# One class of a head's keys and queries loaded and split a slot earlier, in a hybrid RG-LRU and dilated-attention block

## The chip, the cores and the metric

One core of one Trainium2 chip. The metric is the device time of one execution in microseconds (us). Engines are named as in the profile: PE (matmuls) with PEld (its weight loads), DVE, ACT, POOL, and SP, which here only issues DMAs. A change of less than 0.2% (about 4.3 us) is taken as no change.

## The reference

The block is one decoder layer over 2048 positions of width 1024, in float32. Only the attention branch matters here:

```python
DILATED_GROUPS = ((128, 1), (512, 4), (2048, 16))       # window, dilation; 8 heads of 128
h = rms_norm(x, g_norm[l]) * (1.0 + scale[:, None, :]) + shift[:, None, :]
x_rnn, z_rnn, q, k, v, z_attn, g_r, g_a = jnp.split(h @ w_in[l], IN_SPLITS, axis=-1)
...
def dilated_attention_mixture(q, k, v):
    outs, lses = [], []
    for window, dilation in DILATED_GROUPS:
        o, l = dilated_window_attention(q, k, v, window, dilation)   # banded causal softmax
        outs.append(o); lses.append(l)
    w = jax.nn.softmax(jnp.stack(lses, axis=0), axis=0)
    return jnp.einsum("gbsh,gbshd->bshd", w, jnp.stack(outs, axis=0))
...
y_attn = (o * jax.nn.silu(z_attn)) @ w_out_attn[l]
merged = jax.nn.sigmoid(g_r + bg_r) * y_rnn + jax.nn.sigmoid(g_a + bg_a) * y_attn
x = x + gate[:, None, :] * (merged @ w_o[l])             # then a final rms_norm
```

## The kernel before

Every float32 matmul is made of three: an operand is **split** into a high part, a copy rounded to the matmul's format (`hi_act` on ACT, line 160, or `hi_dve`, line 163), and a low part, the difference (`lo_pool` on POOL, line 166, or `lo_dve`, line 169). `mm3` (line 152) then multiplies high with high, high with low and low with high.

The program runs in stages: input projections and the recurrent branch; the attention with the output projection interleaved; then the last products. The change lies in the attention stage. It works on 16 heads (two halves f of the sequence, 8 heads h each), numbered here 0 to 15, and the instruction order of every engine is the order of the code. Time is cut into **slots**. A head has six units, one a slot: four "c" units (a residue class r of the positions modulo 4) and two "w" units (the undilated window), in the order c0, w0, c1, w1, c2, c3. A head starts at its slot B, the next head at B + 6. In each slot the PE does the scores of one unit, then steps of the output projection (the **fill**, matmuls `pj<-yh,S` and `pj<-yl,S`), the transposes of the unit seven slots back, more fill, and the weighted sums of the unit eight slots back:

```python
run(s, HEAD)
...                                   # scores of this slot's unit (PE)
softmax()                             # row minima and exponentials (DVE, ACT)
run(s, SOFTMAX)
owed = spend(fill, owed, rate * 2 / 3)
run(s, EXCHANGE)
owed = spend(fill, owed, rate / 3)
run(s, WEIGHTS)
...                                   # transposes (PE); copies from PSUM and lows (ACT or DVE)
owed = spend(fill, owed, 0.0)
...                                   # weighted sums (PE)
run(s, TAIL)
```

HEAD, SOFTMAX, EXCHANGE, WEIGHTS and TAIL are the five places of a slot at which a head's other work is put, by `at(slot, place, function)` in `enlist`.

The work around the change, for a head that starts at slot B:

- `load_kq(c)` (line 1422) loads the keys and queries of class c into a buffer `kraw` (four of them), by SP's DMA queue.
- `split_kq(c)` splits them into the tile `kq`, of which there is one for all heads; class c is its part c. The high is ACT's (128x512 in the first half, 128x768 in the second), the low POOL's.
- `window_queries(0)` (line 1436), at (B, HEAD), makes two casts on POOL, high and low, of queries of all four classes into the tile `q`. The first "w" unit's scores (matmuls `sc<-kq,q`, slot B + 1) read it.
- `gather` (line 1630), at WEIGHTS of the old head's last slot, is four small ACT instructions that write `sm`. The PE exchanges those statistics between partitions in the next slot (`sc<-sm,msk`), between two score groups. DVE and ACT then work out weights `M` (lines 1648 to 1674).
- `scale` (line 1542) multiplies a unit's probabilities `pp` by `M` on ACT, at the TAIL before the unit's transposes (lines 1562 and 1575, `pT<-cs,pp`).
- `split_v` and `split_v1` split values (`vh`, `wh`) at TAIL, high on ACT and low on POOL; the fill's own operands `yh`, `yl` are split on DVE and POOL. `load_v` and `load_v1` (lines 1442, 1460) load values into three `vraw` buffers.

Of the kernel before, what the change touches and what calls it, by code (L numbers as in the profile page):

```python
# [90 lines left out]
def decoder_block(ctx, tc, x, c, positions, g_norm, w_mod, b_mod, w_in, b_gate, conv_w, conv_b,  # L91
# [1308 lines left out]
    HEAD, SOFTMAX, EXCHANGE, WEIGHTS, TAIL = range(5)  # L1400
    plan, due = {}, []

    def at(slot, place, fn, *args):
        plan.setdefault((slot, place), []).append((fn, args))
# [5 lines left out]
    class Head:  # L1410
# [283 lines left out]
                stored.add((self.f, self.h, i))  # L1694

        def enlist(self, B):
            for c, (ld, s, place) in enumerate(((5, 2, HEAD), (5, 2, SOFTMAX), (4, 1, HEAD), (3, 0, HEAD))):
                at(B - (ld if B else 5), TAIL, self.load_kq, c)
                at(B - s, place, self.split_kq, c)
            at(B, HEAD, self.window_queries, 0)  # L1700
            at(B + 1, EXCHANGE, self.window_queries, 1)
            e = B + NU
            at(e - 1, WEIGHTS, self.gather)
            at(e, HEAD, due.append, self.exchange)
            at(e, SOFTMAX, self.exchange_alone)
            at(e, SOFTMAX, self.maxima)
            at(e, SOFTMAX, self.exponentials)
            at(e, WEIGHTS, self.weights)
            for u, (kind, x) in enumerate(ORDER):
                s = B + u + LAG  # L1710
                at(s - 1, TAIL, self.scale, kind, x)
                at(s - 1, TAIL, self.split_v if kind == "c" else self.split_v1, x)
                at(s - 3, TAIL, self.load_v if kind == "c" else self.load_v1, x)
            e = B + NU + LAG
            at(B + LAG - 1, TAIL, self.load_gate)
            at(e, TAIL, self.merge, 1)
            at(e + 1, TAIL, self.merge, 3)
            at(e + 2, TAIL, self.store)
# [498 lines left out]
```

## Time and profile before

| what | value |
|---|---|
| time, median of 3 runs (range) | 2168.0 us (2166.8 to 2169.54) |
| the profiled execution, its span | 2169.62 us, 2167.8 us |
| mean granted PE clock | 0.998 |
| busy, share of the span: PE, PEld, DVE, ACT, POOL | 99%, 82%, 69%, 60%, 51% |
| attention stage, from the first load of `kraw` to the last scores | 1345 to 1831 us |
| DMA | 521.39 MB, mean 241 GB/s |

A row of the timeline gives start, duration, engine, line, operation, output<-inputs, shapes, how many like it follow each other, and in brackets the idle time of the engine before it with what ended it. A matmul's end is modelled: matmuls follow each other faster than their durations say, so short waits of the PE don't show as idle time. A busy PE is therefore not a PE at its peak.

### The profile page before, as it was taken

To read this page: it belongs to the slowest core of one execution; us is meant where nothing else is said; L and a number is where in the kernel's file an instruction comes from. 1 tells how busy PE (TensorE), PEld (TensorE's weight loads), DVE (VectorE), ACT (ScalarE), POOL (GpSimd) and SP (SyncE) were. 2 spreads that over 40 slices of the span, in tenths; PEclk is the share of its full clock that TensorE was granted. 3 is DMA by queue.
4 is the path that set the end of the run, shared out by engine and by line. 5 is a ranking of instruction groups with operands and counts; after the bars stand their busy time and mean duration, and the time that the engine had idled before them with its cause. 6 is when DMAs were issued, how large, how long until landed. Compare 5 with 4: busy or idle time off the path is not lost.

```text
span 2167.8 us, 32585 instructions
## 1 busy us (share of the span) xinstructions
PE 2138.3 (99%) x10539; PEld 1787.8 (82%) x10539; DVE 1488.1 (69%) x2606; ACT 1296.9 (60%) x2591; POOL 1111.2 (51%) x868
## 2 busy tenths in 40 slices
PE   9999999999999999999999999999999999999998
PEld 6888778888888888888888887888888988878886
DVE  6759878768656725544536584687777787788887
ACT  5748668668644527457548532677878877444333
POOL 1467667777666323223234564466666564422444
PEclk9999999999999999999999999999999999999999
DMA  8467887886655378898996666988887777899553
GB/s 302 144 208 259 277 290 264 285 296 237 175 112 165 108 250 281 295 312 299 323 327 220 163 163 198 288 266 266 269 267 230 242 241 223 298 316 295 183 171 111
DMA packets 416431, 521.39 MB, mean 241 GB/s; under 512 B 107558, under 2 KB 282882, under 8 KB 415236
## 3 DMA queue, kind: packets, MB, share of 16 engines
q1 hardware_dynamic: 376244, 401.65, 59.7%
q10 hardware_dynamic: 34384, 99.78, 12.1%
q0 software_dynamic: 5632, 17.88, 2.6%
q8 instruction: 83, 1.36, 0.3%
q14 instruction: 88, 0.72, 0.1%
HBM read 332.02 MB, written 187.17 MB: 240 GB/s over the span
## 4 chain that ended last, share of the span: by engine, by line
PE 63%; DVE 5%; DMA 5%; POOL 3%; issue 3%; ACT 1%; SPq 1%; POOLq 0%; ACTq 0%; DVEq 0%
PE X L152 13%; PE V L152 13%; PE pj L152 8%; PE Z L152 7%; PE W L152 6%; PE Y L152 6%; PE sc L152 3%; PE o L152 3%; PE pg L152 1%; DMA fg<-mrT 1%; PE pT L1562 1%; POOL kq L166 1%; PE pT L1575 1%; DMA fg<-gaT 1%; DMA oT<-zt 1%
## 5 line engine op out<-in xcount | busy, mean ns | idle before, releaser
L166 POOL TENSOR_TENSOR S<-R,S 128x512 fp32r<-128x512 f32 x192 | 294.3, 1541 | 170.0 <-ACT S L160 87.3
L152 PE MATMUL V<-T,S 128*128 128x512 f32 x1344 | 324.2, 390 | 2.3 <-DVE ev L455 2.3
L152 PE MATMUL X<-T,S 128*128 128x512 f32 x1344 | 323.8, 390 | 1.5 <-ACT u L385 1.3
L152 PE MATMUL pj<-yh,S 128*128 128x512 f32 x896 | 322.1, 403 | 1.3 <-DVE fg L1786 0.8
L152 PEld LDWEIGHTS V<-T,S 128*128 128x128 f32 x1344 | 251.8, 188 | 56.3 <-issue 2.1
L152 PEld LDWEIGHTS X<-T,S 128*128 128x128 f32 x1344 | 251.7, 188 | 56.4 <-ACT u L385 3.0
L166 POOL TENSOR_TENSOR S<-s,S 128x512 fp32r<-128x512 f32 x116 | 170.6, 1471 | 151.1 <-ACT S L160 114.9
L152 PEld LDWEIGHTS pj<-yh,S 128*128 128x128 f32 x896 | 168.5, 188 | 32.6 <-DVE S L169 1.6
L1475 ACT ACTIVATE pp<-pp,st 128x256 f32<-128x256 f32 (+3 forms) x256 | 133.7, 523 | 73.1 <-DVE st L1474 71.7
L152 PE MATMUL pj<-yl,S 128*128 128x512 f32 x448 | 175.9, 393 | 0.6 <-POOL yl L166 0.3
L160 ACT ACTIVATE S<-s 128x512 fp32r<-128x512 f32 x124 | 77.4, 624 | 145.4 <-DVE s L285 91.0
L152 PE MATMUL W<-T,S 128*128 128x512 f32 x672 | 161.6, 389 | 0.0
L152 PE MATMUL Y<-T,S 128*128 128x512 f32 x672 | 161.5, 389 | 0.0
L152 PE MATMUL Z<-T,S 128*128 128x512 f32 x672 | 161.4, 389 | 0.0
L160 ACT ACTIVATE S<-R 128x512 fp32r<-128x512 f32 x200 | 121.6, 623 | 59.0 <-DMA R<-in_w_in_dram 14.8
L169 DVE TENSOR_TENSOR ptl<-pT,pth 128x384 fp32r<-128x384 f32 (+1 forms) x160 | 97.9, 628 | 76.0 <-ACT pth L160 73.7
L152 PEld LDWEIGHTS W<-T,S 128*128 128x128 f32 x672 | 126.0, 188 | 26.9 <-issue 0.9
L152 PEld LDWEIGHTS Z<-T,S 128*128 128x128 f32 x672 | 126.1, 188 | 26.2
L152 PEld LDWEIGHTS Y<-T,S 128*128 128x128 f32 x672 | 126.1, 188 | 26.1
L974 DVE SCALAR_TENSOR_TENSOR xc<-xr,par,xc 128x512 f32<-128x512 f32 x96 | 104.4, 1087 | 58.1 <-ACT xc L968 55.9
L166 POOL TENSOR_TENSOR s<-R,s 128x512 fp32r<-128x512 f32 x32 | 43.2, 1351 | 189.5 <-ACT s L160 173.0
L1542 ACT ACTIVATE pp<-pp,M 128x256 f32<-128x256 f32 (+3 forms) x256 | 117.9, 522 | 22.3 <-DVE M L1674 22.3
(417 smaller groups left out, 4922.8 us busy)
## 6 DMA issues: line engine op xcount, KB each, us to landing
sD<-S ACTq DMA_DIRECT2D x140, 512.0 KB, 3.8
S<-sD SPq DMA_DIRECT2D x140, 512.0 KB, 5.2
S<-wD SPq DMA_DIRECT2D x82, 512.0 KB, 5.6
R<-in_w_in_dram SPq DMA_DIRECT2D x144, 256.0 KB, 3.4
wD<-s ACTq DMA_DIRECT2D x64, 256.0 KB, 5.3
kraw<-kqT SPq DMA_DIRECT2D x32, 384.0 KB, 5.4
T<-in_w_mod_dram SPq DMA_DIRECT2D x16, 512.0 KB, 9.1
vN<-ev SPq DMA_DIRECT2D x32, 256.0 KB, 2.7
```

The lines of the kernel that those rows point to most:

```text
L152: nc.tensor.matmul(o, lhsT=l, rhs=r, start=st, stop=sp, **kw)
L160: nc.scalar.activation(o, i, AF.Copy)
L166: nc.gpsimd.tensor_tensor(o, i, h.bitcast(F32), ALU.subtract)
L169: return nc.vector.tensor_tensor(o, i, h.bitcast(F32), ALU.subtract).ins
L974: nc.vector.scalar_tensor_tensor(xc, xr[:, i : i + CH], cw(i), xc, ALU.mult, ALU.add)
L1475: nc.scalar.activation(pdst, pdst, AF.Exp, bias=m_, scale=-1.0, accum_out=l_)
L1542: nc.scalar.activation(pp, pp, AF.Copy, scale=w)
L1562: nc.tensor.transpose(pt[:, c0 + j * P : c0 + (j + 1) * P], pp[i][:, k * P : (k + 1) * P], ident)
L1575: nc.tensor.transpose(pt[:, c * P : (c + 1) * P], pp[:, half * P : (half + 1) * P], ident)
```

## The change

```diff
         def enlist(self, B):
-            for c, (ld, s, place) in enumerate(((5, 2, HEAD), (5, 2, SOFTMAX), (4, 1, HEAD), (3, 0, HEAD))):
+            for c, (ld, s, place) in enumerate(((5, 2, HEAD), (5, 2, SOFTMAX), (4, 1, HEAD), (4, 1, EXCHANGE))):
                 at(B - (ld if B else 5), TAIL, self.load_kq, c)
                 at(B - s, place, self.split_kq, c)
```

Class 3 of a head's keys and queries is loaded at the TAIL of slot B - 4 instead of B - 3, and split at EXCHANGE of slot B - 1 instead of at HEAD of slot B. Nothing is added or removed; for head 0 the load stays where it was, and no engine's order changes there. The order of PE and DVE is the same throughout.

On ACT, at the border between heads 13 and 14 (the high copy of class 3 is the `kq` row whose source is `kraw_17871` before and `kraw_17784` after; `pp,st` rows are the exponentials of slot B - 1 above and of slot B below). Before:

```order
L1475 ACTIVATE pp_17958,st_17537<-pp_17958,st_17537 128x512
L1630 ACTIVATE sm_17976<-st_17537,cs_60 128x2x16 x4
L160 ACTIVATE pth_17986<-pT_17981 128x512
L160 ACTIVATE pth_17994<-pT_17990 128x384
L1542 ACTIVATE pp_17467<-pp_17467,M_17557 128x384
L1542 ACTIVATE pp_17467<-pp_17467,M_17557 128x512
L160 ACTIVATE vh_18027<-vraw_17869 128x512
L160 ACTIVATE kq_12048<-kraw_17871 128x768
L1475 ACTIVATE pp_18051,st_18041<-pp_18051,st_18041 128x384
```

And now:

```order
L1475 ACTIVATE pp_17958,st_17537<-pp_17958,st_17537 128x512
L160 ACTIVATE kq_12048<-kraw_17784 128x768
L1630 ACTIVATE sm_17978<-st_17537,cs_60 128x2x16 x4
L160 ACTIVATE pth_17988<-pT_17983 128x512
L160 ACTIVATE pth_17996<-pT_17992 128x384
L1542 ACTIVATE pp_17467<-pp_17467,M_17557 128x384
L1542 ACTIVATE pp_17467<-pp_17467,M_17557 128x512
L160 ACTIVATE vh_18029<-vraw_17871 128x512
L1475 ACTIVATE pp_18051,st_18041<-pp_18051,st_18041 128x384
```

The high copy moved ahead of the gather, the copies of transposes, the scales and a value's high copy; the exponentials of slot B have lost it from in front of them.

On POOL at the same border, from class 2's low to the two casts of `window_queries(0)`. Before:

```order
L166 TENSOR_TENSOR kq_12048<-kraw_17782,kq_12048 128x768
L166 TENSOR_TENSOR yl_18006<-R_3429_17838,yh_18005 128x512
L166 TENSOR_TENSOR vh_18027<-vraw_17869,vh_18027 128x512
L166 TENSOR_TENSOR kq_12048<-kraw_17871,kq_12048 128x768
L1436 CAST q_3473_18037<-kq_12048 128x512 x2
```

And now:

```order
L166 TENSOR_TENSOR kq_12048<-kraw_17782,kq_12048 128x768
L166 TENSOR_TENSOR kq_12048<-kraw_17784,kq_12048 128x768
L166 TENSOR_TENSOR yl_18008<-R_3430_17840,yh_18007 128x512
L166 TENSOR_TENSOR vh_18029<-vraw_17871,vh_18029 128x512
L1436 CAST q_3473_18037<-kq_12048 128x512 x2
```

Class 3's low moved ahead of the fill's low and the value's low; the casts have the same instructions ahead of them as before, in another order. On SP the class 3 load stands right behind class 2's, ahead of the other loads of the slot between.

## The prediction

> **What bounds the kernel.** I read the page first, then the stage by windows, the PE's waits in it, the stage's tiles, and last the timeline at the borders between heads.
>
> ```profile
> PE 2138.3 (99%) x10539; PEld 1787.8 (82%) x10539; DVE 1488.1 (69%) x2606; ACT 1296.9 (60%) x2591; POOL 1111.2 (51%) x868
> ```
>
> ```profile
> 1345.00:1840.00 495.00, 485.98 (x3138) 433.87 (x3137) 367.94 (x1066) 381.70 (x1075) 293.99 (x255) 1.00 0.81 256
> ```
>
> The PE is the bound: it is idle for 29.5 us of the span and for 9.0 us of the 495 us of the attention stage (columns: PE, PEld, DVE, ACT, POOL, clock, DMA share). Nothing here can gain more than its waits. Of the PE's waits in that stage these two bear on the change (total, times, longest):
>
> ```profile
> PE sc L152 <- POOL q L1436: 4.6, 5, 1.7
> PE pT L1562 <- ACT pp L1542: 1.0, 2, 0.7
> ```
>
> The first is the wait at which the change aims: a head's first window scores wait for the two casts of the window queries, which stand behind class 3's low. The second is the next in line: transposes that wait for probabilities scaled by the weights M. What the moved pieces cost (min/median/max ns):
>
> ```profile
> L160 ACT ACTIVATE kq<-kraw x64: 614/730/843, 1350.9 to 1803.6; 128x512 fp32r<-128x512 f32 x32, 128x768 fp32r<-128x768 f32 x32
> L166 POOL TENSOR_TENSOR kq<-kraw,kq x61: 1282/1837/2310, 1355.7 to 1805.1; 128x768 fp32r<-128x768 f32 x32, 128x512 fp32r<-128x512 f32 x29
> L1436 POOL CAST q<-kq x60: 603/616/1078, 1378.4 to 1812.2; 128x512 fp32r<-128x512 f32 x60
> ```
>
> **The waits that can go.** The border into head 14 is the worst. First PE, then ACT, POOL and DVE there:
>
> ```profile
> 1763.88 0.38 PE L152 MATMUL sc<-sm,msk 128*128 128x128 f32 x2
> 1770.89 0.50 PE L152 MATMUL sc<-kq,q 128*128 128x256 f32 x2 [1.71 <-POOL q L1436]
> 1771.91 2.09 PE L152 MATMUL sc<-kq,q 128*128 128x256 f32 x10 [0.52 <-POOL q L1436]
> 1775.08 1.08 PE L1562 MATMUL pT<-cs,pp 128*128 128x128 f32 x5
> ...
> 1760.88 0.96 ACT L1630 ACTIVATE sm<-st,cs 128x32 f32<-128x32 f32 x4
> 1764.24 0.84 ACT L160 ACTIVATE kq<-kraw 128x768 fp32r<-128x768 f32 x1
> 1772.71 1.23 ACT L1542 ACTIVATE pp<-pp,M 128x384 f32<-128x384 f32 x2 [3.01 <-DVE M L1674]
> ...
> 1761.69 2.03 POOL L166 TENSOR_TENSOR kq<-kraw,kq 128x768 fp32r<-128x768 f32 x1
> 1765.74 1.30 POOL L166 TENSOR_TENSOR yl<-R,yh 128x512 fp32r<-128x512 f32 x1 [2.02 <-DMA vraw<-vN]
> 1768.25 1.84 POOL L166 TENSOR_TENSOR kq<-kraw,kq 128x768 fp32r<-128x768 f32 x1
> 1770.01 1.85 POOL L1436 CAST q<-kq 128x512 fp32r<-128x512 f32 x2
> ...
> 1762.05 2.22 DVE L169 TENSOR_TENSOR yl<-R,yh 128x512 fp32r<-128x512 f32 x1
> 1768.49 1.88 DVE L163 CAST yh<-R 128x512 fp32r<-128x512 f32 x1
> 1772.50 0.18 DVE L1674 SCALAR_TENSOR_TENSOR M<-M,dm 128x16 f32<-128x16 f32 x1
> ```
>
> ```profile
> 1769.01:1772.43 3.42, 1.20 (x8) 0.85 (x8) 3.32 (x6) 0.70 (x2) 2.85 (x3) 1.00 0.79 255
> 1772.43:1775.84 3.41, 3.41 (x15) 3.01 (x15) 2.65 (x12) 3.13 (x9) 1.30 (x2) 0.50 0.16 58
> ```
>
> The PE's first matmul waits for the high cast, the third for the low one (1.71 and 0.52). A matmul of this form is some 0.28 us long by its modelled end, and ten take 1.46 us undisturbed (next fence), so they start 0.13 apart and each wait hides 0.15 more: 2.5 us lost. After 2.2 us of idle in 3.4 us (3.42 less 1.20) the granted clock was 0.50 for the next 3.41 us: 1.7 us more. Together 4.2 us. The border into head 10:
>
> ```profile
> 1626.95 0.49 PE L152 MATMUL sc<-sm,msk 128*128 128x128 f32 x2
> 1633.39 0.51 PE L152 MATMUL sc<-kq,q 128*128 128x256 f32 x2 [1.05 <-POOL q L1436]
> 1634.41 1.46 PE L152 MATMUL sc<-kq,q 128*128 128x256 f32 x10 [0.51 <-POOL q L1436]
> 1637.28 0.30 PE L1562 MATMUL pT<-cs,pp 128*128 128x128 f32 x1 [0.72 <-ACT pp L1542]
> ...
> 1625.94 0.96 ACT L1630 ACTIVATE sm<-st,cs 128x32 f32<-128x32 f32 x4
> ...
> 1627.41 1.16 DVE L169 TENSOR_TENSOR ptl<-pT,pth 128x512 fp32r<-128x512 f32 x2 [2.02 <-ACT pth L160]
> 1634.83 1.20 DVE L1672 TENSOR_TENSOR M<-M,t__3081_16175 128x16 f32<-128x16 f32 x1
> 1636.35 0.17 DVE L1674 SCALAR_TENSOR_TENSOR M<-M,dm 128x16 f32<-128x16 f32 x1
> ```
>
> Here 1.05 + 0.51 + 0.3 hidden = 1.9 us. The border into head 15:
>
> ```profile
> 1801.27 0.49 PE L152 MATMUL sc<-sm,msk 128*128 128x128 f32 x2
> 1807.50 2.02 PE L152 MATMUL sc<-kq,q 128*128 128x256 f32 x12 [0.86 <-POOL q L1436]
> ...
> 1800.26 0.96 ACT L1630 ACTIVATE sm<-st,cs 128x32 f32<-128x32 f32 x4
> 1806.83 1.18 POOL L1436 CAST q<-kq 128x512 fp32r<-128x512 f32 x2
> ```
>
> 0.86 + 0.15, and twelve matmuls in 2.02 against 1.46 + 2 x 0.13 = 1.72: 1.3 us. In the first half (1345 to 1560 us) the same group has little idle time, and head 6's transposes follow their scale at once:
>
> ```profile
> L152 PE MATMUL sc<-kq,q 128*128 128x256 f32 (+1 forms) x192 | 27.0, 286 | 0.3
> ...
> 1516.19 0.80 ACT L1542 ACTIVATE pp<-pp,M 128x128 f32<-128x128 f32 x2 [1.67 <-DVE M L1674]
> 1516.65 0.83 PE L1562 MATMUL pT<-cs,pp 128*128 128x128 f32 x3
> ```
>
> Idle 0.3, and 0.15 hidden at up to six borders: 0.3 to 1.2; I take 0.9, nearer the top, since a wait under 0.15 doesn't show at all. In sum 4.2 + 1.9 + 1.3 + 0.9 = 8.3 us could go.
>
> **The change part by part.**
>
> *The load.* Fifteen DMA issues move past a few others in SP's queue. It costs nothing: class 3 is still used almost three slots after its issue, and the buffer it takes was emptied a head earlier.
>
> ```profile
> SPq L1460 <- POOL vh L166: 66.0, 24, 7.5
> SPq L340 <- PE pj L152: 45.6, 23, 4.2
> ```
>
> SP waits for value buffers that POOL's lows free; those lows come up to 0.8 us later now. Behind SP's wait stand the fill's weights (line 340), but these already wait 45.6 us for the PE to free their buffers: that is the cover. Without it, a few loads would land 0.8 us late.
>
> *The low on POOL.* The casts keep the same instructions ahead of them. They come earlier only by POOL's idle time, which the low now fills, or where the low waited for ACT's copy. Into head 14: class 2's low ends at 1763.72, DVE's `yl` then gets its turn to 1764.27, class 3's low would take 1.84 to 1766.1, `yl` 1.30 to 1767.9 (its `yh` has to follow the low), `vh` about the same to 1769.2, the casts 2 x 0.61 to 1770.4. The PE's third matmul then starts at 1770.45 instead of 1771.91. The idle time falls well under 2.2 us, so I take it that the clock stays up; ten matmuls and three of the fill (0.7) bring the PE to the transposes at about 1772.5.
>
> *What is late next.* Those transposes need the scale, and the scale needs M at the end of DVE's queue: 1772.68 before. DVE has lost one block (`yh`, 1.88 long behind POOL's 1.84) and got another, since `yh` at 1765 now meets the moved low. I take M 0.2 earlier; bounds 1771.5 (no block) and 1773.4 (0.7 later). Scale 0.62, transposes at 1773.2: 1.9 earlier than 1775.08. With the 0.76 us of half clock after that (0.4), 2.3 us are gained there, not 4.2.
>
> The Trainium skill, "SBUF — State Buffer", section "Who interferes with whom", says that a DVE instruction with two SBUF inputs, or a copy in a two-port mode, and a POOL instruction that reads SBUF exclude each other, the later one waiting whole. `yl` ending 0.55 after class 2's low agrees. It speaks against this change, which puts two lows back to back; by it alone, with DVE never getting between them, M would end at the late bound and the gain there be 1.5 us.
>
> *The high on ACT.* 0.84 us (0.61 in the first half) now stand ahead of the gather, the transposes' copies and the scales. Into heads 10 and 15 the gather ended at 1626.90 and 1801.22, 0.05 before the exchange: the PE now waits 0.79 at each. Into head 14 it ended at 1761.84, 2.04 before it was wanted at 1763.88. Into head 15 the later PE then meets casts 1.0 us earlier: no wait. Net 1.3 - 0.8 = 0.5 gained. Into head 10 the scores no longer wait either, but M decides: DVE had waited 2.02 us for ACT's copy, and this comes 0.84 later, while DVE meets POOL less (line 1672 took 1.20 of M's end behind a low). Bounds: 0.8 lost, 1.1 gained (1.9 - 0.8). I take 0.3 gained, near the middle, since neither the whole shift nor the whole relief is likely. In the first half 0.9, less 0.2 at head 6 where M decides, less 0.3 because M is later there (bounds 0 and 0.6): 0.4.
>
> *Sum:* 2.3 + 0.3 + 0.5 + 0.4 = 3.5 us. The profiled execution took 2169.62 us, 1.8 more than its span and 1.6 above the median: 2166.1 by it, 2164.5 by the median. If part of its excess is that half clock, the median has less to gain; I take 2165.0.
>
> **Rivals.**
>
> 1. *The whole wait goes.* DVE isn't held up, so M comes at its early bound or earlier, and the clock never falls. Gain 8.3, less what the exchange costs where no wait follows, 0.8: 7.5 us, 2160.5. For it: DVE's long `yh` and `yl` beside POOL's low. Against it: ACT idle for 3.01 and DVE for 2.02 us in front of exactly these steps.
> 2. *Slower: the high ahead of the gather.* The copies reach DVE 0.84 late, M follows, and the PE's waits at exchange and transposes bunch within one 3.4 us stretch, so that the clock halves at borders where it did not. Cost: 0.8 into head 10 and 0.6 at head 6 from M; three halved stretches at 1.7 make 5.1; at 14 and 15 gains of 0.9 and 0.5 stay. Net 5.1 slower: 2173. It decides where the idle time in one stretch passes some point between 1.6 (head 10, clock 1.00) and 2.2 us (head 14). The Trainium skill, "TensorE: Matmul & The Clock Gate", section "Why this matters for your kernels", warns only of gaps above about 3 us. The trace differs: 1.71 and 0.52 us were enough. By the page this rival would cost no clock, and end at 2168.
> 3. *Nothing moves.* POOL is behind all the time, and a reordered queue ends when it did: 2168.0. Against it: POOL idle for 2.02 us between class 2's low and the casts.
>
> **How the numbers follow.** My forecast has 0.52, rival 1 0.28, rival 2 0.12, rival 3 0.08. Differences under 0.2%, 4.3 us, cannot be told from none. Forecast and rival 3 lie within; of the forecast's own range (2162.5 to 2168) 0.06 lies beyond 4.3 us. So faster 0.34, same 0.54, slower 0.12. The range reaches to rival 1's 2160.5 and up to 2169.5, past rival 3, and leaves out rival 2 and a little of rival 1.
>
> **What would show it.** The PE's wait for `q` should fall from 4.6 us to under 1.5; `sc<-sm` should show waits for ACT's `sm` near 1627 and 1800, 0.6 to 0.8 each; the wait of `pT` for `pp` should grow from 1.0 to about 2; no stretch near 1772 at clock 0.50. Wrong would be: `pp` waits that stay at 1.0 (rival 1), more than one stretch at 0.50 (rival 2), or casts that still end after 1771 into head 14 (rival 3).

## The result and the profile after

| | before | after |
|---|---|---|
| median of 22 runs each (range), us | 2167.16 (2163.12 to 2170.44) | 2164.48 (2160.84 to 2167.99) |
| ratio, with its 95% interval | | 0.9988 [0.9983, 0.9994] |
| the profiled execution and its span, us | 2169.62, 2167.8 | 2164.76, 2163.0 |

The changed kernel is 2.7 us faster by the medians, 1.3 to 3.7 by the interval. That is less than the 0.2% that counts here as a change, as was forecast, with 2165.0 us forecast and 2164.5 measured.

The page after, with its totals, then the attention stage as one window (PE, PEld, DVE, ACT, POOL, clock, DMA share):

```profile
PE 2136.7 (99%) x10538; PEld 1787.7 (83%) x10539; DVE 1480.0 (68%) x2606; ACT 1296.0 (60%) x2591; POOL 1111.6 (51%) x868
```

```profile
1345.00:1840.00 495.00, 487.19 (x3158) 435.20 (x3157) 361.81 (x1069) 385.08 (x1084) 295.74 (x257) 1.00 0.81 258
```

The PE's idle time in those 495 us fell from 9.0 to 7.8 us. Its waits there, after (total, times, longest):

```profile
PE pT L1562 <- ACT pp L1542: 2.4, 4, 1.6
PE pT L1562 <- DVE ptl L169: 1.3, 2, 0.7
PE pj L152 <- POOL yl L166: 1.0, 3, 0.5
PE sc L152 <- DVE dm L1662: 0.7, 1, 0.7
PE sc L152 <- ACT sm L1630: 0.5, 1, 0.5
PE sc L152 <- POOL q L1436: 0.2, 1, 0.2
```

The wait for the casts, 4.6 us before, is 0.2. The wait for scaled probabilities is 2.4 instead of 1.0, and that for POOL's `yl` 1.0 instead of 0.3. The wait for `dm` is new. That for `sm`, near 1626, is new in this pair of profiles only: two more profiles of the kernel before, listed under the experiments, have one of 0.4 and 0.5 us into head 15.

The spans of the two profiles differ by 4.8 us, but not all of that is the change's. The stage is best measured between two marks of its own. These are the second window scores of heads 1 and 15, before:

```profile
1387.76 1.65 PE L152 MATMUL sc<-kq,q 128*128 128x256 f32 x12
...
1819.12 1.65 PE L152 MATMUL sc<-kq,q 128*128 128x256 f32 x12
```

and after:

```profile
1385.77 1.65 PE L152 MATMUL sc<-kq,q 128*128 128x256 f32 x12
...
1814.75 1.65 PE L152 MATMUL sc<-kq,q 128*128 128x256 f32 x12
```

From the one to the other are 431.36 us before and 428.98 after: 2.4 us are gained in the stage. The first mark is 2.0 earlier already, and so are head 0's first window scores (1356.84 against 1358.83), ahead of which no engine's order has changed; over all profiles shown below it lies anywhere from 1385.6 to 1390.8. So spans of single profiles are not compared here; the length between the marks is. The same marks at every head give the gain border by border (each head's second window scores, after against before, both counted from head 1):

| borders into heads | removable, by the prediction | forecast | measured |
|---|---|---|---|
| 2 to 5 | 0.9, with head 6 | 0.4, with head 6 | +0.4 |
| 6 | | | -1.0 |
| 10 | 1.9 | 0.3 | -0.95 |
| 14 | 4.2 | 2.3 | +2.7 |
| 15 | 1.3 | 0.5 | +1.2 |
| sum | 8.3 | 3.5 | 2.4 |

**The border into head 14, after.** PE, ACT, POOL and DVE in the timeline:

```profile
1769.01 0.45 PE L152 MATMUL sc<-kq,q 128*128 128x256 f32 x2
1769.66 1.46 PE L152 MATMUL sc<-kq,q 128*128 128x256 f32 x10 [0.20 <-POOL q L1436]
1771.77 0.30 PE L1562 MATMUL pT<-cs,pp 128*128 128x128 f32 x1
1772.34 0.87 PE L1562 MATMUL pT<-cs,pp 128*128 128x128 f32 x6 [0.27 <-ACT pp L1542]
...
1771.06 1.23 ACT L1542 ACTIVATE pp<-pp,M 128x384 f32<-128x384 f32 x2 [1.35 <-DVE M L1674]
...
1761.07 4.32 POOL L166 TENSOR_TENSOR kq<-kraw,kq 128x768 fp32r<-128x768 f32 x2
1768.23 1.38 POOL L1436 CAST q<-kq 128x512 fp32r<-128x512 f32 x2
...
1764.66 1.01 DVE L163 CAST yh<-R 128x512 fp32r<-128x512 f32 x1
1768.49 0.64 DVE L163 CAST yh<-R 128x512 fp32r<-128x512 f32 x1
1770.85 0.17 DVE L1674 SCALAR_TENSOR_TENSOR M<-M,dm 128x16 f32<-128x16 f32 x1
```

The lows of classes 2 and 3 now stand in one POOL row (x2). Of the waits of 1.71 and 0.52 us, 0.20 is left. The second `yh` takes 0.64 instead of 1.88, so M ends at 1771.02. The first transpose doesn't wait, and the six behind it wait 0.27 for the second `pp`. No stretch here is at clock 0.50.

**The border into head 10, after:**

```profile
1626.09 0.49 PE L152 MATMUL sc<-sm,msk 128*128 128x128 f32 x2 [0.55 <-ACT sm L1630]
1631.31 1.65 PE L152 MATMUL sc<-kq,q 128*128 128x256 f32 x12
1635.24 0.30 PE L1562 MATMUL pT<-cs,pp 128*128 128x128 f32 x1 [1.59 <-ACT pp L1542]
1635.81 0.87 PE L1562 MATMUL pT<-cs,pp 128*128 128x128 f32 x6 [0.27 <-ACT pp L1542]
...
1632.68 1.28 POOL L166 TENSOR_TENSOR yl<-R,yh 128x512 fp32r<-128x512 f32 x1 [1.67 <-DMA vraw<-vN]
...
1632.81 1.19 DVE L1672 TENSOR_TENSOR M<-M,t__3081_16175 128x16 f32<-128x16 f32 x1
1634.32 0.17 DVE L1674 SCALAR_TENSOR_TENSOR M<-M,dm 128x16 f32<-128x16 f32 x1
```

```profile
1633.31:1636.73 3.42, 1.57 (x10) 1.05 (x9) 3.32 (x8) 1.75 (x3) 1.03 (x2) 1.00 0.51 190
1636.73:1640.14 3.41, 3.41 (x16) 3.18 (x14) 1.76 (x9) 3.08 (x11) 3.40 (x4) 0.50 0.25 72
```

The casts no longer make anything wait, twelve scores run in 1.65 us, and so the PE comes to the transposes 1.9 us before their scale is ready. Four waits of 1.05, 0.51, 0.72 and 0.27 us before, spread out over 5.5 us, have become 1.59 and 0.27 close together: in one stretch the PE is idle for 1.85 us (3.42 less 1.57), and the next one ran at clock 0.50. The border ends 0.95 worse than before. In an execution of the same kernel without the half clock, shown below, it ends 0.6 better, so the half clock costs 1.5 us here.

**The border into head 6, after:**

```profile
1510.96 0.97 PE L152 MATMUL sc<-kq,q 128*128 128x128 f32 x6
1512.64 0.96 PE L152 MATMUL sc<-kq,q 128*128 128x256 f32 x6 [0.71 <-DVE dm L1662]
1515.26 0.84 PE L1562 MATMUL pT<-cs,pp 128*128 128x128 f32 x3 [0.28 <-ACT pp L1542]
...
1505.80 1.52 DVE L163 CAST yh<-R 128x512 fp32r<-128x512 f32 x1
1507.71 1.26 DVE L163 CAST yh<-R 128x512 fp32r<-128x512 f32 x1
1512.33 0.17 DVE L1662 TENSOR_TENSOR dm<-sc,xs 128x16 f32<-128x16 f32 x1
```

The second six scores wait for a PSUM buffer `sc` that DVE's maxima still read. Before, the twelve ran in one row:

```profile
1513.37 1.89 PE L152 MATMUL sc<-kq,q 128*128 128x128 f32 x12
1513.72 0.16 DVE L1662 TENSOR_TENSOR dm<-sc,xs 128x16 f32<-128x16 f32 x1
```

Counted from the start of the exchange (1510.10 before, 1507.69 after), `dm` ended 3.78 us later before and 4.81 after. DVE lost that 1.0 us with the two `yh` copies above, which run beside the moved low (on POOL at 1505.72, for 1.32) and the POOL `yl` behind it (at 1507.40, for 1.29).

### The profile page after: what moved, and what is told of

Its sections match the earlier page's. It is cut to its first block, busy times and chain, and to the rows that moved or that the text cites. A ratio compares the mean times of both kernels' runs of the same rounds, so it can differ in the third digit from the quotient of the medians.

```text
span 2163.0 us, 32592 instructions
## 1 busy us (share of the span) xinstructions
PE 2136.7 (99%) x10538; PEld 1787.7 (83%) x10539; DVE 1480.0 (68%) x2606; ACT 1296.0 (60%) x2591; POOL 1111.6 (51%) x868
## 4 chain that ended last, share of the span: by engine, by line
PE 69%; DVE 5%; DMA 2%; issue 2%; POOL 1%; ACT 1%; SPq 0%; POOLq 0%; ACTq 0%; DVEq 0%
PE X L152 13%; PE V L152 13%; PE pj L152 11%; PE Z L152 7%; PE W L152 7%; PE Y L152 6%; PE sc L152 4%; PE o L152 4%; PE pg L152 1%; PE pT L1562 1%; PE pT L1575 1%; DVE ptl L169 1%; DVE yh L163 1%; DMA kraw<-kqT 1%; DMA meT<-fg 1%
```

## The experiments

Every kernel is timed against the kernel before; 11 runs of the kernel stand against 27 or 33 of before. "Stage" is the length between the two marks in its profile: 431.4 us before, 429.0 after. A stretch of 3.41 us at granted clock 0.50 is called halved. Of the tuple in `enlist` the edits show the last two entries only.

**The load alone.**

```diff
- (4, 1, HEAD), (3, 0, HEAD)
+ (4, 1, HEAD), (4, 0, HEAD)
```

> The load of class 3 a slot earlier, its split at the old place. Theory A (the 2.7 us come from the casts of the window queries, which end earlier): no gain, ratio to the kernel before 1.000 within 0.0007; the PE's wait for q in the attention stage stays at 3 to 5 us, and the casts into head 14 end after 1770 on the clock of the profile before. Rival B (the earlier load matters, through SP's queue or landing times): ratio near 0.9988, and the wait for q falls.

2166.77 us against 2166.79, ratio 0.9998 [0.9989, 1.0007]; stage 431.7. The PE's waits keep their first row:

```profile
PE sc L152 <- POOL q L1436: 4.5, 5, 1.6
```

A stretch at clock 0.50 still begins at 1771.4. The load is worth nothing by itself.

**The split alone.**

```diff
- (4, 1, HEAD), (3, 0, HEAD)
+ (4, 1, HEAD), (3, 1, EXCHANGE)
```

> The split of class 3 at its new place, the load at its old one. Theory A: the whole gain of the changed kernel, ratio 0.9988 within 0.0007, wait for q under 0.5 us, ACT's high copy never waiting for the load. Rival B: ratio near 1.000, or ACT waits for the landing of kraw ahead of the gather.

2165.05 us, ratio 0.9993 [0.9984, 1.0002]; stage 427.5. The interval reaches past 1, so the times alone would not show a gain; the stage does, in a profile that is the fastest of the eleven runs (2161.32). Head by head the gains are those of the whole change (-1.0 at head 6, +2.7 at head 14, +1.2 at head 15), with one exception: into head 10 it gains 0.6, and no stretch is halved there, though the transposes wait as long:

```profile
PE pT L1562 <- ACT pp L1542: 2.5, 4, 1.6
```

```profile
1632.00:1635.41 3.41, 1.73 (x11) 1.09 (x9) 3.31 (x10) 1.22 (x3) 1.28 (x1) 1.00 0.88 292
```

The idle time in the stretch is 1.68 us here, against 1.85 in the profile of the whole change: the stretches begin elsewhere against the work, at 1632.00 and not at 1633.31, and most of the second wait, of 0.27 us, falls into the next one.

**The split behind the gather.** The high copy then no longer stands ahead of `sm`.

```diff
- (4, 1, HEAD), (3, 0, HEAD)
+ (4, 1, HEAD), (4, 1, WEIGHTS)
```

> As the changed kernel, but class 3's split stands behind the gather (place WEIGHTS), still ahead of the transposes' copies and the scales. Theory A (part of the gain is given back where ACT's high copy delays the gather and with it the PE's exchange): the PE's waits for sm at the borders into heads 10 and 15 (0.5 and 0.1 us idle, 0.7 and 0.3 by starts) go; waits of pT for pp stay near 2 us; ratio 0.9984 to 0.9988. Rival C (what is given back comes from M and the halved clock alone, and an earlier arrival at the scores only waits longer behind): ratio 0.9988 as the changed kernel, waits of pT for pp grow by what sm no longer waits.

2163.48 us, ratio 0.9985 [0.9976, 0.9994]; stage 428.5. The wait for `sm` is gone, but not the time: it went to the transposes.

```profile
PE pT L1562 <- ACT pp L1542: 2.8, 4, 2.0
```

Head 6 loses 0.5 instead of 1.0, without a wait for `dm`, and head 15 gains 1.5 instead of 1.2. Into head 10 the loss is 1.1, with a halved stretch from 1641.6. M is what binds there, and where the PE waits for the copy matters little at that border.

**The high alone on ACT, the low where it was.** A `high_kq` and a `low_kq` take the place of `split_kq` for class 3 (the lines below them are numbered 8 higher):

```diff
-                at(B - s, place, self.split_kq, c)
+                if c < 3:
+                    at(B - s, place, self.split_kq, c)
+            at(B - 1, EXCHANGE, self.high_kq, 3)
+            at(B, HEAD, self.low_kq, 3)
```

> Class 3's high copy at its new place on ACT, its low at the old place on POOL, behind the value's low. Theory A (POOL's idle time, filled by the moved low, is what brings the casts forward at the border into head 14; ACT's copy is only a cost): wait for q comes back to 2 to 4 us, at most 1 us less than before, the waits for sm stay, ratio 0.9995 to 1.0008. Rival D (the low waited mainly for ACT's copy): the wait for q falls to under 1 us and the ratio is 0.9990 or less.

2171.13 us, ratio 1.0023 [1.0014, 1.0032]: 4.3 us slower than before, and more than expected. Stage 435.5, and a halved stretch from 1774.2. Its waits:

```profile
PE sc L152 <- POOL q L1444: 5.0, 7, 1.7
PE sc L152 <- ACT sm L1638: 1.1, 2, 0.5
```

Why it is slower shows at the border into head 2 (ACT, then POOL and PE):

```profile
1401.77 0.40 ACT L160 ACTIVATE vh<-vraw 128x256 fp32r<-128x256 f32 x1
...
1402.25 0.74 POOL L166 TENSOR_TENSOR vh<-vraw,vh 128x256 fp32r<-128x256 f32 x1 [1.70 <-ACT vh L160]
1402.95 1.29 POOL L166 TENSOR_TENSOR kq<-kraw,kq 128x512 fp32r<-128x512 f32 x1
1404.19 1.16 POOL L1444 CAST q<-kq 128x512 fp32r<-128x512 f32 x2
1404.85 2.01 PE L152 MATMUL sc<-kq,q 128*128 128x128 f32 x12 [0.16 <-POOL q L1444]
```

The high copy moved ahead of the value's high copy on ACT, so that POOL's low of the value waits 1.70 us for that one instead of 1.33, with class 3's low and the casts in line behind. Into head 11 it is the same, with 3.37 instead of 2.77. At these borders the low didn't wait for its own copy: having the copy early makes the casts later as long as POOL's order stays. The other borders, of which most lose 0.2 to 0.6 us, were not followed one by one. The gain of the change comes from POOL's order, from the low that fills POOL's idle time ahead of the value; the early high copy is only what allows it, and by itself a cost.

**The weights sooner.** With the casts out of the way M is next, so here `weights` (the work of DVE and ACT up to M) goes to SOFTMAX of its slot, ahead of the fill's splits: first on the changed kernel, then on the kernel before.

```diff
-            at(e, WEIGHTS, self.weights)
+            at(e, SOFTMAX, self.weights)
```

> The changed kernel, with the weights M worked out right behind the exponentials (place SOFTMAX instead of WEIGHTS), so that DVE does them ahead of the fill's splits. Theory A (after the change the transposes wait for M, which DVE reaches late, and the clock halves behind that wait): the waits of pT for pp fall from 2.4 to under 0.5 us, no stretch at half clock near 1636, and against the kernel before the ratio is 0.9970 to 0.9982. Rival C (the PE would be held anyway, by DVE's earlier wait for ACT's exponentials or by the fill's own splits, which now come later): the waits of pj for yh or yl grow by as much and the ratio stays at 0.9988 or above.

> The kernel before, with M worked out right behind the exponentials and nothing else. Theory A: the waits of pT for pp (1.0 us) go, the waits for q stay at 3 to 5 us with the half clock into head 14, ratio 0.9988 to 1.0000: M is a limit mainly once the casts are not. Rival C: if DVE's order alone was the cause of the late border into head 14, the wait for q falls there too and the ratio is 0.9980 or less.

On the changed kernel: 2163.97 us against 2166.73, ratio 0.9985 [0.9976, 0.9995]; stage 427.5, no halved stretch, no row for `pp` among the waits, and head 6 loses 0.5 instead of 1.0. In place of that wait others stand:

```profile
PE pT L1562 <- DVE ptl L169: 1.7, 3, 0.7
PE sc L152 <- ACT sm L1630: 1.0, 2, 0.5
```

On the kernel before: 2166.48 us, ratio 0.9998 [0.9989, 1.0007]. The wait for the casts shrinks but remains:

```profile
PE sc L152 <- POOL q L1436: 3.2, 3, 1.5
```

So M and the casts are separate waits in a row: with the casts late, M early is worth nothing that the times show. The first ratio was expected lower. Moving M takes away the wait on `pp` and the halving. Head 10 then gains 0.05 where the split alone gained 0.6, and the stage is no shorter than with the split alone (427.5 each), so apart from the halving the wait that went is made up for elsewhere. The rows above make the copies that DVE now does later a likely place, but this is not shown. One thing stays open: in its profile the stage of the second kernel is 429.0 us long, 2.4 less than before and without a halved stretch, but its times show no gain. The profiled execution took 2163.74 us, the least of its eleven; one profile doesn't say how often the others are halved.

**Both together**: the split at WEIGHTS and the weights at SOFTMAX.

> Both: class 3 loaded and split early but behind the gather, and M right behind the exponentials. Theory A: no wait for sm, q or pp of over 0.5 us in the attention stage, ratio 0.9965 to 0.9978, the fastest of all. Rival C: no better than the changed kernel, 0.9988, with new waits of the PE elsewhere in the stage.

2163.21 us, ratio 0.9985 [0.9976, 0.9994]; stage 427.05, the shortest here. The longest of the PE's waits left in the stage:

```profile
PE pT L1562 <- DVE ptl L169: 1.6, 3, 0.7
PE pj L152 <- POOL yl L166: 1.1, 3, 0.5
PE pj L152 <- DVE fg L1786: 1.0, 1, 1.0
```

None of the four waits of this case (`q`, `sm`, `pp`, `dm`) shows any more, among the shorter ones either. This kernel has the lowest median of all, 3.5 us under before, but less was gained than expected, and its interval doesn't separate it from the change as it is (0.9988).

**Does one kernel always halve at the same border?** The two kernels again, twice each, for their profiles alone.

> The changed kernel again, one look. Theory A (the clock halves for one stretch of 3.41 us when the PE was idle for more than about half of the stretch before, and the stretches run on by themselves, so it depends on where their borders fall): near the transposes into head 10 the waits are as before, 1.5 to 2 us of idle time, and the clock is halved behind them only where 1.7 us or more of it fall into one stretch; no half clock into head 14. Rival E (the halving belongs to the kernel): half clock into head 10 in every profile of it.

> The same kernel and the same expectations: by theory A the half clock into head 10 may be there or not, by rival E it is there each time.

> The kernel before again. Theory A: waits for q of 1.7 and 0.5 us into head 14 as before; the halved stretch is there only where a border doesn't cut that wait in two. Rival E: half clock into head 14 each time.

> The same kernel and the same expectations as the run before it.

| profile | us | stage, us | halved in the stage |
|---|---|---|---|
| before: first, second, third | 2169.62, 2170.31, 2169.94 | 431.4, 431.8, 431.8 | into head 14, each |
| after: first | 2164.76 | 429.0 | into head 10 |
| after: second | 2168.15 | 429.0 | into head 10 |
| after: third | 2163.46 | 427.5 | none |

The kernel before halves into head 14 each time, and so do the load alone and the high alone, in one profile each. None of the seven profiles with the low moved does: three of the changed kernel, and one each of the split alone, the split behind the gather, the weights sooner on the changed kernel, and both together. The changed kernel halves into head 10 in two of three. The third gains 0.6 at that border, as the split alone did. The stage got 3.2 us shorter on the mean of three and three, and the medians of the timed runs say 2.7. Of the second profile's 2168.15 us, 6.8 ran at half clock near 300 us, far ahead of the change; its own marks show the same stage as the first.

Whether a stretch is halved goes, in the stage, with the idle time of the PE in the stretch ahead. Second profile of before, then third of after:

```profile
1769.56:1772.98 3.42, 1.65 (x11) 1.45 (x12) 3.28 (x8) 0.43 (x2) 2.22 (x3) 1.00 0.89 286
1772.98:1776.38 3.40, 3.40 (x14) 2.96 (x13) 2.05 (x10) 3.40 (x12) 1.92 (x3) 0.50 0.04 13
```

```profile
1635.02:1638.43 3.41, 1.69 (x10) 1.42 (x11) 3.31 (x10) 1.89 (x4) 1.02 (x2) 1.00 0.36 147
1638.43:1641.85 3.42, 3.42 (x23) 3.13 (x22) 1.77 (x8) 3.42 (x12) 2.95 (x4) 1.00 0.32 94
```

1.77 us idle and halved; 1.72 and not.

## Why the prediction was right, and where its terms were not

The time and the sign came out as forecast, and the mechanism too: the casts stop holding the window scores, M becomes the next limit, and the gain is much less than the 8.3 us that could go. The sum (3.5 against 2.4 in the profile it was made for, and 3.2 by three profiles of each) was right with terms that erred both ways, by +1.1 and -2.2 us in that profile. That these half cancelled is luck. So is some of the closeness of 2165.0: it was counted from a median of 2168.0 over three runs, which over 22 is 2167.2.

- *Into head 14: forecast 2.3, measured 2.7.* M was taken 0.2 earlier, between bounds of 1771.5 and 1773.4. In its profile the PE reaches the slot before this border 0.5 us earlier than before, so its 1771.02 is 1771.5 by the times before: M came at its early bound, because DVE's last `yh` was not held up any more. The casts ended at 1769.61, or 1770.1 so counted, 0.3 before the 1770.4 that was worked out. By the rule of the Trainium skill, "SBUF — State Buffer", section "Who interferes with whom", M would have ended at the late bound if DVE got no turn between the two lows. The trace agrees with the exclusion and not with that outcome: DVE did get its turn. Its `yl` was held by the first low and done before the second, which is why the two took 4.32 us instead of 2 x 1.84, and the next `yh` waited for the second one's end (1.01 above). At head 6 the same exclusion cost more, with the 1.26 us of a `yh` beside POOL's `yl`.
- *Into head 15: forecast 0.5, measured 1.2.* The error is the exchange, put down with 0.8 us of waiting. It shows no wait after the change, and the PE went from the scores ahead of it to the exchange in 0.85 us against 0.68: 0.2. The forecast moved the gather by the copy's whole length and let the rest of ACT stand, but ACT's exponentials, which wait for DVE's minima, came 0.45 earlier after their scores (1798.80 less 1795.48 before, 1795.20 less 1792.33 after) and took up most of it. The other two profiles of before are 0.5 slower at this border, with waits for `sm` of their own; against these the change gains 1.7.
- *Into head 10: forecast 0.3, measured -0.95 with the halved stretch and 0.6 without it.* The waits were judged right, with 0.55 us at the exchange (0.6 to 0.8 forecast) and 1.9 at the transposes. The step that failed is the clock: no stretch was expected to be halved. It is the mechanism of the second rival, at one border of the three it needed, and its condition, a point between 1.6 and 2.2 us of idle time, was right.
- *The first half: forecast 0.4, measured -0.6.* Borders 2 to 5 gave the 0.4. Head 6 was to lose 0.2 by a late M and lost 1.0. M, which is made from `dm`, came 1.0 later: it ended 6.06 us after the start of the exchange before (1516.16) and 7.09 after it now (1514.78). The transposes still wait for `pp` at the end, so the step that failed here is M's, sized too small. On the way lies a wait that the working did not have, for the PSUM buffer that DVE's maxima read. Where M is early (the weights sooner on the changed kernel) that wait is left, without one for `pp`, and 0.5 is lost. DVE's block was looked for only on the way to M, not on the way to that buffer.

Of the signs named ahead, the wait for `q` (0.2, under 1.5), the wait for `pp` (2.4, about 2) and the full clock near 1772 came as said. Waits for `sm` were to be two and were one, 0.5 near 1626. That the load costs nothing was right; its time moved by 0.0 when done alone.

The first rival (all of it goes, 2160.5) fell, since `pp` and `dm` took over. The third fell too: POOL did fill its idle time. The most that any kernel here gained, with the split behind the gather and the weights sooner, is 4.3 us of stage, not 7.5.

## What to carry to other kernels

When a wait on one engine's queue is to go, ask for the order of that queue, not for the operand's age: the same copy made early cost 4.3 us without the low's move behind it and gained 2.7 with it. Then look for what else the displaced engines hold up, buffers of PSUM as well as operands, and at what spacing the remaining waits fall: two short waits that come together can cost more in granted clock than the longer waits that they replace. Where such a gain is near the spread of the runs, measure it between two marks inside the changed stage, over several profiles of each kernel.

## What the runs showed of the hardware

**The clock and scattered idle time.** The granted clock moves in stretches of 3.41 us which run on by themselves, not in step with the work: into head 10 a stretch began 1.9 us ahead of the first transpose in one profile of the changed kernel (1633.31, 1635.24) and 3.0 us ahead in that of the split alone (1632.00, 1635.05). In the stage a stretch at 0.50 followed one with 1.77 us or more of idle PE (1.77, 1.84, 1.85, 1.88, 2.14, 2.22), and none followed 1.42, 1.68 or 1.72, though no single gap was longer than 2.0 us. That is about half of a stretch, in pieces. Outside the stage it doesn't hold as well. Near 298 us two stretches with 1.76 and 1.77 us idle were not followed by a halved one. Near 27 us three were, after only 0.9 to 1.1 of idle time (third profile of before, the high alone, the weights sooner on the kernel before); some of the PE's work there is matmuls of 128x1. So idle time by the records is not the whole condition, and what else belongs to it stays open. The Trainium skill, "TensorE: Matmul & The Clock Gate", section "Why this matters for your kernels", warns of gaps above about 3 us; here shorter ones in sum were enough. A halved stretch cost 1.5 us at the border into head 10 (0.6 gained without it, 0.95 lost with it), a little under half of its length. Since the stretches run freely, the same kernel had it in two executions and not in a third.

**A tiny DVE instruction behind a POOL low.** The row of line 1672 (two SBUF inputs, 128x16) took 1.19 us while POOL's 128x512 `yl` ran beside it; rows of its size in the same chain take 0.17. It starts at 1632.81 and ends at 1634.00, just behind that `yl` (1633.96). It took 1.20 already before the change, at the same place, and it stands on the way to M. So 1.0 us of the wait for M into head 10 comes from where POOL puts that low.
